# Three edits at the end of a mixture-of-experts kernel: one final store, a w2 load in three pieces, and eight small reads of x

## The chip, the cores and the metric

The kernel runs on one core of one Trainium2 chip. The metric is device time in microseconds (us) of one execution. A core has a matmul engine (PE), three engines for elementwise work (DVE, ACT, and POOL, which here mostly issues DMAs), a queue engine (SP), and 16 DMA engines that move data between the chip's main memory (HBM) and its on-chip memory (SBUF). DMAs issued from SP and ACT go to hardware queues (q1 and q10 in the profile), those issued from POOL to a software queue (q0).

## What is computed

Eight experts, each a two-layer network on its own 256 tokens:

```
x: [8, 256, 512]   w1: [8, 512, 2048]   w2: [8, 2048, 512]   all float32
h   = maximum(x @ w1, 0)
out = h @ w2            # [8, 256, 512] float32
```

## The kernel before

The loads convert float32 to bf16 on the way, so all weight traffic is issued by POOL (`load_w1`, L82; `load_w2`, L88). Weights come in whole experts: a w1 of one expert and a w2 of one expert are 4 MB each in HBM and 2 MB in SBUF. x comes with two plain loads on SP for experts 0 and 1 (L67, cast by DVE at L69), and then in pairs of experts from POOL (L74). The list `loads` holds the order: w1 and w2 of expert 0, x of 2 and 3, w1 and w2 of expert 1, and so on; L104 puts w1 of the last expert ahead of w2 of the one before it. `issue` takes from that list as far as it is told to. The order of PE's and POOL's instructions is the order in which the code issues them (`manual_schedule`, L179); those of the other engines are placed by a scheduler.

Two w2 loads are cut along the rows that a partition holds (`PIECES`, L55): expert 6 into 8 and 8 rows of 512, expert 7 into 4, 4, 4, 2 and 2. A row here is a slice of k of the second matmul. Each partition's part of a piece is one packet, so a piece is 128 packets, eight for each DMA engine, and each DMA leaves sixteen completion marks, one for each engine.

For each expert, PE transposes x (`prepare`, L119), runs layer 1 (`layer1`, L135: 64 matmuls of 128 x 256 into PSUM, with ReLU by ACT at L142), and layer 2 (`layer2`, L161: 32 matmuls of 128 x 512 into two PSUM tiles, one for each half m of the tokens). For experts 6 and 7 layer 2 goes over k outside and m inside, so that it can begin with the first piece of w2. Layer 1 of expert 7 runs ahead of layer 2 of expert 6.

DVE copies the results out of PSUM (L172); the very last one, m = 1 of expert 7, is copied by ACT (L170). Outputs are gathered in SBUF by groups of experts: 0 to 2, 3 to 6, and 7 alone. The group of 0 to 2 is stored from POOL in the midst of the loads (`store`, L92), that of 3 to 6 from POOL after all loads (L201, 2 MB). Expert 7 is stored in two halves: m = 0 from SP after DVE's copy, m = 1 from ACT after ACT's copy (L175). On SP's queue stand only the two x loads and that half store.

Of the kernel before, what the change touches and what calls it, by code (L numbers as in the profile page):

```python
# [9 lines left out]
FP32 = mybir.dt.float32  # L10
# [4 lines left out]
def kernel(  # L15
# [7 lines left out]
    nc = tc.nc  # L23
    P = 128
    E, C, H = x.shape
    F = w1.shape[2]
    MC = C // P
# [8 lines left out]
    out_v = out.rearrange("e (p mo) k -> e p (mo k)", mo=MC)  # L36
# [4 lines left out]
    x_pool = ctx.enter_context(tc.tile_pool(name="x_pool", bufs=2))  # L41
# [10 lines left out]
    identity = const.tile([P, P], BF16, name="identity")  # L52


    PIECES = {E - 2: [8, 8], E - 1: [4, 4, 4, 2, 2]}  # L55


    GROUPS = [(0, 1, 2), (3, 4, 5, 6), (7,)]
    GROUP = {e: g for g in GROUPS for e in g}
# [3 lines left out]
    xbs, w1s, w2s, outs = {}, {}, {}, {}  # L63
# [20 lines left out]
    def load_w2(e):  # L84
        w2s[e] = t = w2_pool.tile([P, K2 * H], BF16, name="w2_sb")
        k = 0
        for n in PIECES.get(e, [K2]):
            nc.gpsimd.dma_start(t[:, k * H:(k + n) * H], w2_v[e, :, k * H:(k + n) * H])  # L88
            k += n

    def store(g):
        nc.gpsimd.dma_start(  # L92
            og_v[:, g[0]:g[-1] + 1, :], outs[g][:].rearrange("p e m h -> p e (m h)")
        )
# [11 lines left out]
    def issue(upto):  # L106
        while loads:
            f, e = loads[0]
            if (f, e) not in upto:
                break  # L110
            loads.pop(0)
            f(e)

    def prepare(e):
        xb = xbs[e]
        xt_ps = psum_t.tile([P, K1, MC, P], BF16, name="xt_ps")
        for ko in range(K1):
            for mo in range(MC):
                nc.tensor.transpose(xt_ps[:, ko, mo, :], xb[:, mo, :, ko], identity[:])  # L119
        xT = xT_pool.tile([P, K1, C], BF16, name="xT")  # L120
        nc.vector.tensor_copy(  # L121
            xT[:].rearrange("p k c -> p (k c)"),
            xt_ps[:].rearrange("p k m q -> p (k m q)"),
        )
        return xT

    def layer1(e, xT):
        w1_r = w1s[e][:].rearrange("p (ko q j) -> p ko q j", ko=K1, j=K2)
        hT = hT_pool.tile([P, K2, C], BF16, name="hT")
        for pr in range(K2 // 2):  # L130
            h_ps = psum_h.tile([P, 2, C], FP32, name="h_ps")
            for s in range(2):
                j = pr * 2 + s
                for ko in range(K1):
                    nc.tensor.matmul(  # L135
                        h_ps[:, s, :],
                        w1_r[:, ko, :, j],
                        xT[:, ko, :],
                        start=(ko == 0),
                        stop=(ko == K1 - 1),  # L140
                    )
            nc.scalar.activation(  # L142
                hT[:, pr * 2:pr * 2 + 2, :].rearrange("p a c -> p (a c)"),
                h_ps[:].rearrange("p a c -> p (a c)"),
                mybir.ActivationFunctionType.Relu,
            )
        return hT

    def layer2(e, hT):
        last = e == E - 1  # L150
        g = GROUP[e]
        if e == g[0]:
            outs[g] = out_pool.tile([P, len(g), MC, H], FP32, name=f"out_sb{g[0]}")
        out_sb = outs[g][:, e - g[0]]
        o_ps = [psum_o.tile([P, H], FP32, name="o_ps") for _ in range(MC)]
        if e in PIECES:
            order = [(k, m) for k in range(K2) for m in range(MC)]
        else:
            order = [(k, m) for m in range(MC) for k in range(K2)]
        for k, m in order:  # L160
            nc.tensor.matmul(  # L161
                o_ps[m][:],
                hT[:, k, m * P:(m + 1) * P],
                w2s[e][:, k * H:(k + 1) * H],
                start=(k == 0),
                stop=(k == K2 - 1),
            )
            if k == K2 - 1:
                if last and m == 1:
                    nc.scalar.copy(out_sb[:, m, :], o_ps[m][:])  # L170
                else:
                    nc.vector.tensor_copy(out_sb[:, m, :], o_ps[m][:])  # L172
                if last:
                    eng = nc.scalar if m == 1 else nc.sync
                    eng.dma_start(out_v[e, :, m * H:(m + 1) * H], out_sb[:, m, :])  # L175

    load_x_first(0)
    load_x_first(1)
    with tc.manual_schedule(engines={mybir.EngineType.PE, mybir.EngineType.Pool}):  # L179
        f, e = loads.pop(0)  # L180
        f(e)
        make_identity(nc, identity)
        f, e = loads.pop(0)
        f(e)
        make_identity(nc, identity)
        issue([(load_w2, 0), (load_x, X_GROUPS[0]), (load_w1, 1), (load_w2, 1), (load_w1, 2)])
        xT = prepare(0)
        for e in range(E - 1):
            issue(
                [(load_w2, e + 2), (load_w1, e + 3), (load_w1, E - 1), (load_w2, e + 1)]  # L190
                + [(load_x, g) for g in X_GROUPS if g[0] <= e + 4]
            )
            for g in GROUPS[:-2]:
                if g[-1] == e - 1:
                    store(g)
            hT = layer1(e, xT)
            xT = prepare(e + 1)
            if e == E - 2:
                hT_last = layer1(E - 1, xT)
            layer2(e, hT)  # L200
        store(DEFER)  # L201
        layer2(E - 1, hT_last)
# [28 lines left out]
```

## Time and profile before

| | us |
|---|---|
| median of 4 runs (lowest, highest) | 182.69 (182.31, 182.73) |
| the profiled execution | 182.43 |
| its span, first to last instruction | 180.6 |
| PE busy with matmuls | 131.4 (73%) |
| DVE, ACT, POOL busy | 17.1, 40.1, 16.5 |
| layer 2, matmul of 128 x 512, count and busy | 256, 56.7 |
| loads of w, 2 MB each in SBUF: median from issue to landing | 61.4 |
| HBM read, written | 71.30 MB, 4.19 MB |

Each number of the profile is from one execution, the profiled one. Busy time is time in which an engine had an instruction in work; a line of the timeline gives start, duration, engine, source line and operation, and in brackets how long the engine sat idle before it and what ended that wait. The page's row "DMA" gives for 40 equal slices of the span the busy share of the 16 DMA engines in tenths, and "PEclk" the share of its full clock that PE was granted.

### The profile page before, as it was taken

How to read it: one execution, taken by the hardware profiler on the slowest of the kernel's cores; microseconds unless marked ns; L12 is line 12 of the kernel's file. 1: busy time of each engine (PE TensorE's matmuls, PEld its weight loads, DVE VectorE, ACT ScalarE, POOL GpSimd, SP SyncE). 2: the span in 40 equal slices, each digit the busy share in tenths (PEclk: the TensorE clock that was granted, in tenths of full speed). 3: DMA queues.
4: the chain of work that ended last, by engine and by line, in shares of the span. 5: the costliest groups of instructions: out<-in, count | busy, mean ns of one | idle time of the engine just before them, and what ended most of it. 6: DMA issues, size and time to landing. Idle time of an engine off the chain costs nothing.

```text
span 180.6 us, 1861 instructions
## 1 busy us (share of the span) xinstructions
PE 131.4 (73%) x832; PEld 92.1 (51%) x832; DVE 17.1 (9%) x25; ACT 40.1 (22%) x66; POOL 16.5 (9%) x34
## 2 busy tenths in 40 slices
PE   0206999169894999349894999539995997887960
PEld 0105874059543874139642884127942897833420
DVE  0300011100111011100111002100031001000210
ACT  2001440016300450006300360003600264600010
POOL 7601011010000023000201002010100101000100
PEclk9999999969999699969999699975999699999996
DMA  6998999899999989989998999999899989999995
GB/s 220 245 229 181 229 232 218 189 232 232 200 207 232 225 173 241 232 185 221 232 229 185 225 196 232 210 232 232 185 221 232 229 180 366 220 207 214 208 395 211
DMA packets 5351, 40.48 MB, mean 224 GB/s; under 512 B 480, under 2 KB 480, under 8 KB 3296
## 3 DMA queue, kind: packets, MB, share of 16 engines
q0 software_dynamic: 4768, 38.80, 97.7%
q1 hardware_dynamic: 432, 1.31, 2.0%
q10 hardware_dynamic: 144, 0.26, 0.4%
q8 instruction: 6, 0.10, 0.2%
q14 instruction: 1, 0.01, 0.0%
HBM read 71.30 MB, written 4.19 MB: 418 GB/s over the span
## 4 chain that ended last, share of the span: by engine, by line
DMA 70%; another core or an unknown queue 11%; PE 11%; POOL 2%; issue 2%; ACT 0%; POOLq 0%
DMA w_sb<-in_w_dram 46%; DMA xb<-in_x_dram 24%; PE o_ps L161 6%; PE h_ps L135 5%; POOL w_sb L82 1%; POOL w_sb L88 1%; POOL xb L74 0%; ACT out_sb L170 0%; POOL identity masks.py:199 0%; POOL identity masks.py:197 0%; PE xt_ps L119 0%; POOLq masks.py:199 0%; POOLq L88 0%; POOLq L215 0%
## 5 line engine op out<-in xcount | busy, mean ns | idle before, releaser
L135 PE MATMUL h_ps<-xT,w_sb 128*128 128x256 bf16 x512 | 70.9, 310 | 33.3 <-DMA w_sb<-in_w_dram 33.3
L135 PEld LDWEIGHTS <-w_sb 128*128 128x128 bf16 x512 | 63.1, 150 | 42.6 <-DMA w_sb<-in_w_dram 36.7
L142 ACT ACTIVATE hT<-h_ps 128x512 bf16<-128x512 f32 x64 | 38.2, 597 | 117.8 <-PE h_ps L135 117.8
L161 PE MATMUL o_ps<-w_sb,hT 128*128 128x512 bf16 x256 | 56.7, 379 | 5.0 <-DMA w_sb<-in_w_dram 5.0
L161 PEld LDWEIGHTS <-hT 128*128 128x128 bf16 x256 | 24.9, 98 | 34.5 <-issue 6.2
L172 DVE COPY out_sb<-o_ps 128x512 f32<-128x512 f32 x15 | 10.3, 691 | 59.0 <-PE o_ps L161 59.0
L121 DVE COPY xT<-xt_ps 128x1024 bf16<-128x1024 bf16 x8 | 5.5, 691 | 94.3 <-PE xt_ps L119 94.3
L88 POOL DMA_DIRECT2D w_sb<-in_w_dram x13 | 7.0, 536 | 76.0 <-DMA w_sb<-in_w_dram 73.8
L119 PE MATMUL xt_ps<-identity,xb 128*128 128x128 bf16 x64 | 5.3, 230 | 4.9 <-DVE xb L69 4.9
L82 POOL DMA_DIRECT2D w_sb<-in_w_dram x8 | 4.8, 600 | 29.8 <-PE h_ps L135 17.8
L119 PEld LDWEIGHTS <-xb 128*128 128x128 bf16 x64 | 4.7, 117 | 4.9 <-DVE xb L69 4.9
L74 POOL DMA_DIRECT2D xb<-in_x_dram x3 | 2.1, 717 | 28.0 <-PE xt_ps L119 28.0
L170 ACT COPY out_sb<-o_ps 128x512 f32<-128x512 f32 x1 | 0.6, 586 | 16.6 <-PE o_ps L161 16.6
L92 POOL DMA_DIRECT2D out_dram<-out_sb x2 | 1.5, 756 | 18.7 <-DVE out_sb L172 17.7
L69 DVE CAST xb<-x_sb 128x1024 bf16<-128x1024 f32 x2 | 1.4, 694 | 4.7 <-DMA x_sb<-in_x_dram 4.7
L142 ACT ACT_TABLE_LOAD x1 | 1.3, 1283 | 0.7 <-PEq L215 0.7
masks.py:199 POOL TENSOR_SCALAR_AFFINE_SELECT identity<-identity 128x128 bf16<-128x128 bf16 x2 | 0.6, 287 | 0.2
masks.py:197 POOL MEMSET identity<- 128x128 bf16 x2 | 0.4, 223 | 0.0
L215 POOL MEMSET const-float32-0.0<- 128x1 f32 x1 | 0.1, 98 | 0.2 <-issue 0.2
L215 POOL MEMSET const-bfloat16-1.0<- 128x1 bf16 x1 | 0.1, 101 | 0.0
L215 POOL MEMSET const-uint8-127<- 128x1 uint8 x1 | 0.1, 101 | 0.0
L215 POOL MEMSET const-float32-1.0<- 128x1 f32 x1 | 0.1, 98 | 0.0
## 6 DMA issues: line engine op xcount, KB each, us to landing
w_sb<-in_w_dram POOLq DMA_DIRECT2D x14, 2048.0 KB, 61.4
w_sb<-in_w_dram POOLq DMA_DIRECT2D x2, 1024.0 KB, 57.5
out_dram<-out_sb POOLq DMA_DIRECT2D x1, 2048.0 KB, 9.9
xb<-in_x_dram POOLq DMA_DIRECT2D x3, 512.0 KB, 43.9
out_dram<-out_sb POOLq DMA_DIRECT2D x1, 1536.0 KB, 64.5
w_sb<-in_w_dram POOLq DMA_DIRECT2D x3, 512.0 KB, 47.8
x_sb<-in_x_dram SPq DMA_DIRECT2D x2, 512.0 KB, 3.8
w_sb<-in_w_dram POOLq DMA_DIRECT2D x2, 256.0 KB, 27.5
```

Of the source, the lines that this page charges most:

```text
L69: nc.vector.tensor_copy(b[:].rearrange("p m q k -> p (m q k)"), t[:])
L74: nc.gpsimd.dma_start(t[:].rearrange("p e m q k -> p e (m q k)"), xg_v[:, g[0]:g[0] + 2, :])
L82: nc.gpsimd.dma_start(w1s[e][:], w1_v[e])
L88: nc.gpsimd.dma_start(t[:, k * H:(k + n) * H], w2_v[e, :, k * H:(k + n) * H])
L92: nc.gpsimd.dma_start(og_v[:, g[0]:g[-1] + 1, :], outs[g][:].rearrange("p e m h -> p e (m h)"))
L119: nc.tensor.transpose(xt_ps[:, ko, mo, :], xb[:, mo, :, ko], identity[:])
L121: nc.vector.tensor_copy(xT[:].rearrange("p k c -> p (k c)"), xt_ps[:].rearrange("p k m q -> p (k m q)"),)
L135: nc.tensor.matmul(h_ps[:, s, :], w1_r[:, ko, :, j], xT[:, ko, :], start=(ko == 0), stop=(ko == K1 - 1),)
L142: nc.scalar.activation(hT[:, pr * 2:pr * 2 + 2, :].rearrange("p a c -> p (a c)"), h_ps[:].rearrange("p a c -> p (a c)"), mybir.ActivationF ...
L161: nc.tensor.matmul(o_ps[m][:], hT[:, k, m * P:(m + 1) * P], w2s[e][:, k * H:(k + 1) * H], start=(k == 0), stop=(k == K2 - 1),)
L170: nc.scalar.copy(out_sb[:, m, :], o_ps[m][:])
L172: nc.vector.tensor_copy(out_sb[:, m, :], o_ps[m][:])
```

## The change

Three edits. Expert 7's w2 is loaded in pieces of 8, 4 and 4 rows. Its output is stored by one DMA from SP, after both halves are copied. And once expert 4's layer 2 is issued, `small_loads` takes a buffer of the pool that x's first two loads used, writes 16 rows of it with a DVE copy out of expert 4's result, and then issues eight reads from SP into the same rows: 15 rows of x (2 KB each), then 14, and so on down to 8. Each read waits for the one before it, the first for the DVE copy. The change is described as reads on 15 down to 8 DMA engines. What is read is used by nothing.

```diff
-    PIECES = {E - 2: [8, 8], E - 1: [4, 4, 4, 2, 2]}
+    PIECES = {E - 2: [8, 8], E - 1: [8, 4, 4]}
...
                 else:
                     nc.vector.tensor_copy(out_sb[:, m, :], o_ps[m][:])
-                if last:
-                    eng = nc.scalar if m == 1 else nc.sync
-                    eng.dma_start(out_v[e, :, m * H:(m + 1) * H], out_sb[:, m, :])
+        if last:
+            nc.sync.dma_start(out_v[e], out_sb.rearrange("p m h -> p (m h)"))
+
+    def small_loads(e):
+        t = x_pool.tile([P, MC * H], FP32, name="x_sb")
+        nc.vector.tensor_copy(t[:16, 0:H], outs[GROUP[e]][:16, e - GROUP[e][0], 0])
+        for k in range(15, 7, -1):
+            nc.sync.dma_start(t[:k, 0:H], x[0, :k, :])
...
             layer2(e, hT)
+            if e == 4:
+                small_loads(e)
         store(DEFER)
         layer2(E - 1, hT_last)
```

As built, DVE's small copy stands between expert 4's two copies out of PSUM, and SP's queue holds the two x loads, the eight reads and the final store, in that order. Counts and order on PE are unchanged; POOL issues two DMAs fewer, ACT one fewer.

## The prediction

> **What bounds the kernel now.** I read the page's row of DMA shares and its list of queues first, then the timeline of the last 30 us, the waits of SP's queue, and last the trace's records of single DMA packets and of the sixteen completion marks that each DMA leaves.
>
> ```profile
> PEclk9999999969999699969999699975999699999996
> DMA  6998999899999989989998999999899989999995
> ...
> q0 software_dynamic: 4768, 38.80, 97.7%
> q1 hardware_dynamic: 432, 1.31, 2.0%
> q10 hardware_dynamic: 144, 0.26, 0.4%
> q8 instruction: 6, 0.10, 0.2%
> ```
>
> The DMA engines are busy from the first slice to the last, nearly all of it (97.7%) with the software queue that POOL issues to: every load of w1, w2 and grouped x, and the two grouped stores. Work that is not on this path is free as long as it stays off it. The timeline of the tail:
>
> ```profile
> 158.74 3.61 PE L161 MATMUL o_ps<-w_sb,hT 128*128 128x512 bf16 x16 [1.34 <-DMA w_sb<-in_w_dram]
> ...
> 163.61 7.07 PE L161 MATMUL o_ps<-w_sb,hT 128*128 128x512 bf16 x32 [1.25 <-DMA w_sb<-in_w_dram]
> ...
> 168.63 0.76 POOL L92 DMA_DIRECT2D out_dram<-out_sb  x1 [17.66 <-DVE out_sb L172]
> 170.98 3.61 PE L161 MATMUL o_ps<-w_sb,hT 128*128 128x512 bf16 x16 [0.31 <-DMA w_sb<-in_w_dram]
> ...
> 174.42 0.69 DVE L172 COPY out_sb<-o_ps 128x512 f32<-128x512 f32 x1 [6.09 <-PE o_ps L161]
> 174.63 0.59 ACT L170 COPY out_sb<-o_ps 128x512 f32<-128x512 f32 x1 [16.59 <-PE o_ps L161]
> 175.13 0.35 SPq L175 DMA_DIRECT2D out_dram<-out_sb  x1
> 175.25 0.37 ACTq L175 DMA_DIRECT2D out_dram<-out_sb  x1
> ```
>
> PE and the copies are done at 175.2, yet the span is 180.6. The page's chain follows PE and ACT here, but the packets say what the last 5 us are: the grouped store of experts 3 to 6 (2 MB, issued at 168.63) stands in each engine's queue behind the last w2 piece. It drains on the first engine at 176.45 and on the last at 178.12; only then do the final stores' packets run there, and they end at 179.42. So the end is one DMA engine's queue, not PE.
>
> That queue is not equally long everywhere. The sixteen marks of the last w2 piece fall between 171.8 and 173.5. Following each engine's packets by their period shows why: each of the six q8 packets (16 KB of instructions) hit a different engine, and each put that engine back by about 1.1 us for good. At the end ten engines lie 0 to 0.6 us behind the first, two 1.2 to 1.3, and four 1.6 to 1.7. These four set the end; the ten have at least 1.0 us to spare.
>
> **The change, part by part**, on those four engines.
>
> Last w2 as 8, 4, 4 instead of 4, 4, 4, 2, 2. Packet periods on one engine: 606 ns in an 8-row piece (from expert 6's halves), 304 in a 4-row piece, 154 in a 2-row piece, eight packets each, plus 21 ns for the mark. Before: 3 x (8 x 304 + 21) + 2 x (8 x 154 + 21) = 9.87 us. After: (8 x 606 + 21) + 2 x (8 x 304 + 21) = 9.78 us. Gain 0.1 us.
>
> One store of 512 KB instead of two of 256 KB. Before, 16 packets of 2 KB at 80 ns and two marks of 6 ns: 1.29 us. After, 8 packets of 4 KB at the 155 ns of the grouped store and one mark: 1.25 us. Gain 0.05 us. ACT loses an issue of 0.37 us, which nothing waits for.
>
> What these two edits push back is PE's end. The 8-row piece lands at 163.56 + 4.87 = 168.43 (before, the first 4-row piece was there at 166.02), and all 32 matmuls come after it: 32 x 0.221 (7.07 us / 32) = 7.1, so PE ends at 175.6, not 174.6. Copies to 176.2; then one SP issue that waits for both. SP's x load issued at 0.74 had its first packet at 1.75, and the final store's first packet came 1.33 us after its issue, so the store's packets are at the engines 177.2 to 177.6. The cover is the grouped store, which keeps the four late engines busy until 178.0. It covers by 0.4 us; if that cover were gone, each further microsecond of PE would be a microsecond of time. The early engines run dry for up to 1 us, and end about 179.1, still ahead.
>
> The small reads. DVE's copy of 16 x 512 lies in a DVE idle of 2.76 us between its copies at 111.93 and 115.38: nothing. Then eight reads on SP, of 15 down to 8 rows of 2 KB, each waiting for the one before, since they write the same tile. Queued behind them on SP is only the final store:
>
> ```profile
> SPq L175 <- DVE out_sb L172: 173.5, 1, 173.5
> SPq L226 <- DMA out_dram<-out_sb: 3.9, 3, 2.8
> ```
>
> SP has nothing to do from 1.6 to 175.1. From issue to landing the HBM transfers on the hardware queues take 3.8 us (x, 512 KB) to 4.5 (256 KB store). At 4.5 the eight end at 112.6 + 36 = 149. They may take up to (176.2 - 112.6) / 8 = 7.9 us each before the final store is late. So SP is covered.
>
> What is not covered is engine time: each read puts one 2 KB packet and a mark into a queue that is never empty. If one row goes to one engine, always counted from the same engine, eight engines get all eight reads and the other eight get 7 down to none; if the change doesn't do what its description says and the rows go round, it is 92 / 16 = 5.75 each. The price of one insertion is not in the trace. From below: a 2 KB packet and its mark in the final stores, 0.086 us, with no gap at the handover. From above: an instruction packet put its engine back by 1.09 us where an equal amount of the same queue takes half of 1.208, so 0.49 us of insertion, plus 0.09: 0.58 us. Nothing below zero: the reads remove no packet. I take 0.09, since the final stores are the nearer row in kind and size; eight of them are 0.7 us, and by the upper end 4.6.
>
> Does it land on a late engine? Six of sixteen are late, four of them decide, and the trace doesn't name engines. If the late ones lay at random, all four would miss the eight fully loaded engines in 70 of 1820 draws; if six late ones lie side by side, in about one start in five. So I take it that a deciding engine gets seven or eight. The last w2 piece, PE's end and the grouped store are then late by the same 0.7, so the cover of 0.4 stays.
>
> Sum: -0.1 - 0.05 + 0.7 = +0.55 us. The profiled execution took 182.43 (span 180.6 and 1.83 around it), which gives 182.98; the median of four runs is 182.69, 0.26 above it, and carries to **183.24**.
>
> The Trainium skill ("DMA: Bandwidth & Descriptors", section "Why a DMA increments its semaphore by 16 and not by 1") says that a hardware-queue DMA on k engines uses the lowest-numbered k, which would make engines 0 to 7 the fully loaded ones; no row here shows an engine's number. The same page ("Queues, rings and completion order") says that an engine takes turns between its queues packet by packet. The row disagrees in part: on the four late engines the grouped store's packets ran on unbroken from 176.5 to 178.0 while the final stores already ran elsewhere. By the rule the reads slip in and the sum stands; by the row they would wait for the software queue to run dry, which is the third rival.
>
> **Rivals.**
>
> 1. Not slower: the late engines are those with few reads. Its place is the gap between engines: an engine with 0.6 us of lag can take (1.66 - 0.6) / 8 = 0.13 us a read before it becomes the last. If the four late engines hold none to three of the reads (at most 0.26 us) and an insertion costs under 0.13, the sum is -0.15 to +0.1: 182.5 to 182.8. It decides as soon as no late engine has more than three. For it: the ten others do have 1.0 us to spare. Against: the odds above.
>
> 2. Insertion costs like the instruction packets, 0.2 to 0.58 us a read: +1.5 to +4.5, so 184.2 to 187.2. For it: the only packets seen to break into the software queue cost this. Against: they were 16 KB, and handovers between queues elsewhere took 6 ns.
>
> 3. The reads wait until the software queue is dry, at about 178, and the final store stands behind them on SP: eight at 2.5 us (3.8 less 1.25 of transfer) and a store of 4: about 20 us more, 203. For it: three handovers in this trace (x to software queue at 4.6, grouped store to SP's store, SP's to ACT's on the late engines) all ran one queue dry first. Against: the instruction packets got in amid a backlog.
>
> 4. The tail's cover fails (late first packet or a slow last piece): +0.2 to +0.8, on top of the sum; to 184.0.
>
> 5. Faster by more than the edits add up to: the disturbance at 145 to 147.5, where every engine lost 0.04 to 0.9 us without a cause in this trace, falls elsewhere. Up to -0.6: 182.1.
>
> **How the numbers follow.** Forecast 45%, with rival 4 in it 8% more; rival 1 19%; rival 2 14%; rival 3 5%; rival 5 9%. A difference of 0.2% is 0.37 us, about what measuring this kernel can tell from none. Slower by more: forecast less its lower edge (38 of 45), rivals 2, 3, 4: 65%; rounded to 0.62 for what rival 1 may take. Faster by more: rival 5, and rival 1 where packets and store save twice what I gave: 0.16. Within: 0.22. The forecast's own range is 182.9 to 183.9. The whole reaches down to 182.2, which holds rival 1, and up to 184.8, which holds the cheaper half of rival 2; rival 3, rival 2's upper half and some of rival 5 are left out.
>
> **What would show it.** In the new profile: SP's queue with eight issues spaced under 8 us and ended before 150; the marks of the last w2 piece spread wider by 0.7 us and later than 173.5 by 0.6; PE's end at 176.2 or so, with no wait for DMA before its last matmuls; one final store whose packets on the last engine follow the grouped store's without a gap. The forecast is wrong if those marks are no later than before (rival 1), later by over 1.3 us (rival 2), or if the eight issues run past 176 (rival 3).

## The result

| | before | after |
|---|---|---|
| median of all runs, us (runs) | 182.57 (63) | 182.94 (43) |
| ratio, 95% interval | | 1.0021 [1.0015, 1.0027] |
| the profiled execution, us | 182.43 | 183.33 |
| its span, us | 180.6 | 181.5 |

The change makes the kernel 0.37 us slower; the forecast was 0.55 slower, which lies above the interval of 0.27 to 0.49 us. The profiled execution after is the slowest of its 43 runs, so the two spans differ by more than the kernels do: the sizes below come from the ratios, the profiles show only where things lie.

The page's DMA row and queue list of the kernel after:

```profile
DMA  6999999999999999999999999999999999999994
...
q0 software_dynamic: 4480, 38.80, 97.0%
q1 hardware_dynamic: 616, 1.76, 2.6%
q8 instruction: 6, 0.10, 0.2%
```

The software queue moved the same 38.80 MB in 288 packets fewer (the 4- and 2-row pieces), q10 (ACT's queue) is gone, and q1 holds the reads and the one store. Still no slice in which the DMA engines rest.

The timeline of the tail after (start, duration, engine, line, operation, idle before it):

```profile
164.33 3.61 PE L161 MATMUL o_ps<-w_sb,hT 128*128 128x512 bf16 x16 [1.25 <-DMA w_sb<-in_w_dram]
...
169.20 7.07 PE L161 MATMUL o_ps<-w_sb,hT 128*128 128x512 bf16 x32 [1.25 <-DMA w_sb<-in_w_dram]
169.35 0.76 POOL L92 DMA_DIRECT2D out_dram<-out_sb  x1 [38.13 <-DVE out_sb L172]
176.09 0.69 DVE L172 COPY out_sb<-o_ps 128x512 f32<-128x512 f32 x1 [7.03 <-PE o_ps L161]
176.30 0.59 ACT L170 COPY out_sb<-o_ps 128x512 f32<-128x512 f32 x1 [17.59 <-PE o_ps L161]
176.91 0.38 SPq L174 DMA_DIRECT2D out_dram<-out_sb  x1
```

All 32 matmuls of expert 7 now run without a gap behind the 8-row piece, and PE ends at 176.27 in place of 174.59. The store's first packet is at 177.78. SP's timeline and waits after:

```profile
0.74 0.85 SPq L67 DMA_DIRECT2D x_sb<-in_x_dram  x2
113.40 43.00 SPq L180 DMA_DIRECT2D x_sb<-in_x_dram  x8
176.91 0.38 SPq L174 DMA_DIRECT2D out_dram<-out_sb  x1
```

```profile
SPq L180 <- DVE x_sb L178: 109.3, 1, 109.3
SPq L180 <- DMA x_sb<-in_x_dram: 42.9, 8, 6.7
SPq L174 <- DVE out_sb L172: 20.4, 1, 20.4
```

The eight reads are issued from 113.4 to 156.1, 5.1 to 7.0 us apart. Each leaves as many completion marks as it has rows, 15 down to 8, one on each engine that it uses. Then SP waits 20.4 us for the copies: the final store doesn't wait for the reads.

The completion marks show who sets the end. Each line holds the sixteen marks of one DMA in order of time, in us, taken from the trace's records:

```
before, grouped store   176.87 176.99 177.00 177.04 177.05 177.21 177.27 177.28 177.32 177.40 178.05 178.12 178.39 178.42 178.46 178.48
before, ACT's store     178.14 178.28 178.29 178.30 178.31 178.49 178.56 178.59 178.64 178.70 179.32 179.38 179.66 179.70 179.73 179.76
after, grouped store    177.24 177.32 177.39 177.52 177.59 177.60 177.65 177.67 177.70 177.93 178.56 178.91 178.92 178.94 178.97 179.10
after, final store      179.38 179.40 179.41 179.42 179.45 179.46 179.47 179.48 179.52 179.56 179.79 180.14 180.17 180.18 180.20 180.35
```

Ten engines and six late ones, before and after. After, the ten finish the final store together (179.38 to 179.56): they had run dry and waited for its first packet. The late ones finish one store's length, 1.24 us, behind their own grouped store: they never ran dry. The last of them sets the end, 0.6 us later than before in these two executions.

### The profile page after: what moved, and what is told of

It reads as the page before. It is cut to its first block, busy times and chain, and to the rows that moved or that the text cites. A ratio compares the mean times of both kernels' runs of the same rounds, so it can differ in the third digit from the quotient of the medians.

```text
span 181.5 us, 1870 instructions
## 1 busy us (share of the span) xinstructions
PE 127.2 (70%) x832; PEld 89.7 (49%) x832; DVE 17.5 (10%) x26; ACT 40.1 (22%) x66; POOL 15.4 (8%) x32
## 3 DMA queue, kind: packets, MB, share of 16 engines
q0 software_dynamic: 4480, 38.80, 97.0%
## 4 chain that ended last, share of the span: by engine, by line
PE 61%; DMA 19%; another core or an unknown queue 15%; POOL 1%; issue 1%; ACT 0%; POOLq 0%
PE h_ps L135 32%; PE o_ps L161 27%; DMA w_sb<-in_w_dram 19%; PE xt_ps L119 1%; POOL xb L74 0%; POOL w_sb L82 0%; ACT out_sb L170 0%; POOL identity masks.py:199 0%; POOL identity masks.py:197 0%; POOL w_sb L88 0%; POOLq masks.py:199 0%; POOLq L222 0%
## 5 line engine op out<-in xcount | busy, mean ns | idle before, releaser
L135 PE MATMUL h_ps<-xT,w_sb 128*128 128x256 bf16 x512 | 66.4, 297 | 35.1 <-DMA w_sb<-in_w_dram 35.1
L135 PEld LDWEIGHTS <-w_sb 128*128 128x128 bf16 x512 | 60.6, 148 | 42.4 <-DMA w_sb<-in_w_dram 38.5
L88 POOL DMA_DIRECT2D w_sb<-in_w_dram x11 | 5.9, 535 | 57.9 <-DMA w_sb<-in_w_dram 55.7
L82 POOL DMA_DIRECT2D w_sb<-in_w_dram x8 | 4.8, 596 | 31.3 <-PE h_ps L135 18.3
```

Of the source, the lines that this page charges most:

```text
L82: nc.gpsimd.dma_start(w1s[e][:], w1_v[e])
L135: nc.tensor.matmul(h_ps[:, s, :], w1_r[:, ko, :, j], xT[:, ko, :], start=(ko == 0), stop=(ko == K1 - 1),)
```

## The experiments

Times are ratios to the kernel before on the same chip, with 95% intervals; 0.001 is 0.18 us.

**The tail edits alone**: the call of `small_loads` left out.

```diff
-            if e == 4:
-                small_loads(e)
```

> The changed kernel without the eight reads: 8, 4, 4 pieces and one store alone. Theory (one late DMA engine's queue sets the end; the reads are the cost, the tail edits save packets): 0.15 us faster than before. Rival A (the tail edits are the cost: PE now ends about 1.1 us later and the store comes late to engines that run dry; the reads fall on engines with time to spare): 0.3 to 0.4 us slower than before, like the whole change. In the trace by the theory: PE ends near 175.6, the store's first packets near 177.2, its last ones on the late engines right behind the grouped store.

Measured 0.9987 [0.9975, 0.9999]. The same kernel again, with the last runs below:

> The tail edits alone once more, for a second interval and on the same chip as the others of this call: 0.1 to 0.3 us faster than before.

Measured 0.9993 [0.9979, 1.0006]. The mean of the two is 0.18 us faster; rival A, which wanted 0.3 to 0.4 slower, falls. The tail in its first profile:

```profile
168.20 7.07 PE L161 MATMUL o_ps<-w_sb,hT 128*128 128x512 bf16 x32 [1.25 <-DMA w_sb<-in_w_dram]
...
175.92 0.35 SPq L174 DMA_DIRECT2D out_dram<-out_sb  x1
```

PE ends at 175.27, 0.7 us later than in the profile before, and the kernel is no slower for it.

**The reads alone**: the kernel before, with `small_loads` and its call.

> The kernel before with the eight reads alone. Theory: +0.5 to +0.7 us (a late engine gets seven or eight reads at 0.09 us). Rival A: 0 to +0.1 us. Rival B (a read costs more than 0.09 us on an engine, and the late engines get only some of them): +0.5 as well, but the q0 packets of one engine show gaps of over 0.2 us where a read goes in.

Measured 1.0025 [1.0015, 1.0036], +0.46 us. So the reads are the cost, and tail edits and reads add up: -0.18 + 0.46 = +0.28 is within the interval of +0.37, at its lower end. A read does not leave gaps of over 0.2 us: see the marks of the next run.

**Reads on all engines**: eight reads of 16 rows, tail edits kept.

```diff
-        for k in range(15, 7, -1):
+        for k in [16] * 8:
```

> The changed kernel with eight reads of 16 rows each, so that all sixteen engines get all eight. Theory: the deciding engines already got seven or eight, so the time is that of the changed kernel or up to 0.1 us more: +0.4 to +0.6 us against before. Rival B (the deciding engines got only some of the reads): 0.3 us or more above the changed kernel, +0.7 or more against before.

Measured 1.0039 [1.0026, 1.0052], +0.71, which is 0.89 over the tail edits alone. That is 0.34 above the change itself, as rival B wants it; the two intervals just touch (1.0026 and 1.0027), so the times alone don't quite exclude my theory. The price of one read can be read off the marks of the 2 MB loads. With the tail edits alone a load into which no instruction packet falls takes 9.68 or 9.69 us on nearly every engine, mark to mark; in this run 9.78 where one read falls into it and 9.87 where two do. So a read costs 0.09 to 0.095 us on its engine, and eight cost 0.70 to 0.75.

**Reads on half of the engines**: eight reads of 8 rows.

```diff
-        for k in range(15, 7, -1):
+        for k in [8] * 8:
```

> The changed kernel with eight reads of 8 rows each, so that only eight engines get any. Theory: if the deciding engines are among those eight, the same as the changed kernel, +0.4 us against before; if none of them is, the reads are free and the time is that of the tail edits alone, 0.15 us faster than before. In the trace the marks of a DMA late in the run must fall into two halves 0.7 us apart, apart from the lag of the instruction packets.

Measured 1.0012 [1.0002, 1.0021], +0.22, which is 0.40 over the tail edits alone: neither full nor free. The marks say why. When the reads begin, four engines are late, by 1.09, 1.09, 1.34 and 1.39 us; over the load of expert 5's w2, into which two reads fall, two of them take 9.69 and two 9.87. So two of the four get the reads, the less late ones, and two get none. At the end:

```
grouped store, rows of 8   177.00 177.14 177.15 177.18 177.46 177.51 177.52 177.53 177.58 178.02 178.12 178.16 178.22 178.30 178.69 178.72
```

Two engines stand out at 178.7. Without their eight reads (0.70 to 0.75 us) they would be at about 178.0, and the last would be the one at 178.30. In this execution the cost is therefore the 0.42 by which they pass it. The time agrees (0.40, to within some 0.25), but the reads on four engines below weaken that agreement.

**Reads on twelve engines**: eight reads of 12 rows, edited like the two before.

> The changed kernel with eight reads of 12 rows each. Eight on all sixteen engines gave +0.95 us over no reads, eight on eight engines +0.46. If reads fall on the engines counted from one fixed end and the late engines that eight rows spare are among the next four: +0.95 over no reads, so +0.7 us against before. If they are among the last four: +0.46, so +0.2 against before. If the engines of a read rotate: three quarters of 0.95, +0.5 against before.

Measured 1.0041 [1.0026, 1.0056], +0.75, 0.93 over the tail edits: as much as on all sixteen. In its marks three of the four engines late by then take 9.87 us over the load with two reads, and one 9.69. The intervals alone would also allow that the engines rotate (+0.5); the marks don't, since of these four three got each of the first three reads and the fourth none. Which engines are late need not be the same as in the execution with 8 rows (see the account of the prediction), so the step from two to three of four doesn't place a given engine.

**Reads on four engines**: eight reads of 4 rows.

> The changed kernel with eight reads of 4 rows each. Theory (a read costs 0.115 us on each engine that it uses and matters only where it falls on a late engine): either the late ones among the first eight engines are among the first four, then as with eight rows, +0.2 us against before, or they aren't, then the reads are free and the time is that of the tail edits alone, 0.2 us faster than before. Rival (the reads cost something by being there at all, through the memory or SP): more than the tail edits alone in any case, in proportion to the rows: +0.46 x 4 / 8 = 0.23 over them.

Measured 1.0013 [1.0001, 1.0026], against 0.9993 [0.9979, 1.0006] for the tail edits on the same chip, 0.36 us more. The intervals touch. Against the mean of the two tail runs, the baseline of the other runs here, it is 0.42 more, as much as with 8 rows. In the marks none of the four engines late by then gets a read (9.69 us a load), so by the theory these reads should have been free; its profiled execution ends its grouped store at 178.42, the two of the tail edits at 178.10 and 178.60. Whether four engines' reads cost anything is not settled. The rival of a cost by being there, forecast at 0.23, is not excluded, and some of the cost of the other runs may be of that kind.

**Sixteen reads of 16 rows**, from expert 1 on.

```diff
-        for k in range(15, 7, -1):
+        for k in [16] * 16:
...
-            if e == 4:
+            if e == 1:
```

> Sixteen reads of 16 rows, from expert 1 on, tail edits kept. Theory: the cost goes with the number of reads on the deciding engine: 16 x 0.115 = 1.84 us over the tail edits alone, +1.6 against before. Rival (a fixed cost, or one that later work takes back): about what eight such reads cost, +0.7 against before. Issues about 6 us apart, so that SP is through by 160.

Measured 1.0081 [1.0068, 1.0094], +1.48, so 1.66 over the tail edits alone, 0.104 us a read, to within some 0.02. The cost goes with the number and nothing later takes it back; that all of it is a fixed cost is out.

**The cover at the tail taken away**: tail edits, no reads, last w2 in two pieces of 8.

```diff
-    PIECES = {E - 2: [8, 8], E - 1: [8, 4, 4]}
+    PIECES = {E - 2: [8, 8], E - 1: [8, 8]}
```

> The tail edits without reads, and the last w2 in two pieces of 8: 16 matmuls (3.6 us) stand behind the last piece, so PE ends near 176.9 and the store's packets come near 178.6, when the grouped store has left even the late engines (178.0). Theory (the late engines' grouped store covers PE's lateness, by some 0.4 to 1 us): the cover is gone, and the time is 0.4 to 0.9 us above the tail edits alone, which were 0.24 us faster than before: +0.2 to +0.7 us. Rival (PE's end doesn't matter, the store's packets alone do): 0.3 us faster than before.

Measured 1.0028 [1.0013, 1.0043], +0.51, 0.69 over the tail edits with 8, 4, 4. Its tail:

```profile
173.04 3.61 PE L161 MATMUL o_ps<-w_sb,hT 128*128 128x512 bf16 x15 [1.45 <-DMA w_sb<-in_w_dram]
...
176.47 0.69 DVE L172 COPY out_sb<-o_ps 128x512 f32<-128x512 f32 x1 [8.64 <-PE o_ps L161]
176.69 0.58 ACT L170 COPY out_sb<-o_ps 128x512 f32<-128x512 f32 x1 [19.11 <-PE o_ps L161]
177.30 0.35 SPq L174 DMA_DIRECT2D out_dram<-out_sb  x1
```

PE ends at 176.65, the store's first packet is at 178.14, when the grouped store has left even the late engines (177.99). All sixteen marks of the final store lie within 0.18 us, 179.75 to 179.93: now the store's issue sets the end for every engine.

**The tail edits one by one.** The pieces alone, two half stores kept:

> The kernel before with expert 7's w2 in pieces of 8, 4, 4 alone, two half stores kept. Theory: 0.1 us faster than before (9.78 us of packets on each engine in place of 9.87), or the same; PE ends about 1 us later and this costs nothing. Rival (the saving of the tail edits is all in the single store): no difference.

Measured 0.9997 [0.9984, 1.0011]. The single store alone, pieces 4, 4, 4, 2, 2 kept:

> The kernel before with one final store alone, pieces 4, 4, 4, 2, 2 kept. Theory: 0.05 us faster than before, so no difference that can be told, and up to 0.1 more if a second store has a cost of its own after its last packet. Rival (the saving of the tail edits is all here): 0.2 us faster.

Measured 0.9995 [0.9978, 1.0013]. Both are too small for these intervals; neither theory nor rival is told apart here.

**The reads put later**: after expert 5 in place of expert 4.

> The changed kernel with its reads put after expert 5 in place of expert 4. The reads then start near 135 and, at about 6 us each, end near 178 to 183, while SP's final store is ready at 176.9. Theory (SP's queue is covered only as long as the reads are through before 176): the store is late by 1 to 6 us and the time goes up by as much, less the 1.1 us for which engines are still busy then: +1 to +5 us against before. Rival (the reads get quicker as the pieces get smaller, and are through in time): +0.4, as in the changed kernel.

Measured 1.0034 [1.0019, 1.0048], +0.62, not told apart from the change. SP's timeline:

```profile
135.63 36.55 SPq L180 DMA_DIRECT2D x_sb<-in_x_dram  x8
177.19 0.38 SPq L174 DMA_DIRECT2D out_dram<-out_sb  x1
```

My expectation was wrong: the reads get quicker as the software queue's packets get smaller, 5.8 and 6.4 us apart at first, 4.3 to 4.8 among the last four. What shrinks is mostly the time after a read's first packet: on its engine the read's mark often goes out only after one more packet of the software queue, 1.30 us behind the read where these are 16 KB, 0.4 in the 4-row pieces. The last issue is over at 172.2, and the store goes out when the copies are done. SP's cover holds even with the reads put 22 us later.

## Why the prediction was right, and where it was off

**What sets the end**: right. One late DMA engine's queue does, before and after; the grouped store's cover for PE's lateness is shown by the run that takes it away (0.69 us). The cover was wider than the 0.4 of the prediction: after the change the final store's first packet is at 177.78, 0.87 us after its issue, and the grouped store's last packet on the latest engine ends at 178.77, 1.0 us behind it. So rival 4 falls.

**The tail edits**: -0.15 forecast, -0.18 as the mean of two runs. PE's end with the reads was forecast at 175.6 plus the reads' delay, 176.2 or so, and lay at 176.27. That closeness is partly luck: two profiles of one kernel, the tail edits, have PE's end 0.47 us apart (175.27 and 175.74).

**Price of one read**: right. 0.09 taken, 0.09 to 0.095 by the marks, 0.104 by sixteen reads to within 0.02. The upper bound of 0.58, from the instruction packets, is far off for a 2 KB packet: rival 2 falls.

**Which engines get them**: this is the step that was mis-sized. "So I take it that a deciding engine gets seven or eight", 0.7 us; the reads cost 0.46 alone and 0.55 on top of the tail edits, the worth of five to six. With 8 rows two of the first four late engines get all eight, but they are not the latest ones, and the lead of some 0.3 us that the latest had on them swallows nearly half of the price. In the changed kernel's own marks three of the four engines that are late when the reads begin get both the 15-row and the 14-row read, and the fourth, the latest then, gets the 15-row read and not the next. At the end of that execution the last engine is one that took neither the 9-row nor the 8-row read (4.867 us for each 8-row piece of expert 6, where the two late ones that took them have 4.961); those two end 0.2 us before it.

Nor need the late engines be the same in every execution. The six instruction packets that make engines late last 893, 893, 948, 945, 935 and 975 ns in the profile with 8 rows, 948, 945, 935, 975, 974 and 961 in that with 12, and 974, 962, 893, 893, 951 and 945 in the changed kernel's. All fourteen profiles show the same round of eight lengths to within some 15 ns, begun at one of four places. If a length goes with an engine, which fits the late engines that got reads in these three profiles but was not tested, other engines are late in other executions, and the "five to six" is a mean over them. Rival 1 named the mechanism, time to spare, but wanted the late engines to have at most three reads.

**SP's queue**: the reads were through at 161.7, not 149: 6.1 us from issue to landing, not at most 4.5. The margin I gave, 7.9 us each, held, so it cost nothing.

**The reads behind the software queue** (rival 3): wrong. They broke into a full queue, the first packet of each 3.3 to 4.0 us after its issue, where SP's first x load needed 1.0. That agrees in kind with the rule of the Trainium skill ("DMA: Bandwidth & Descriptors", section "Queues, rings and completion order") that an engine takes turns between its queues packet by packet. The turn doesn't come at once, though, and the wait is not a number of packets: with the reads put later it is 3.3 to 3.4 us too where the software queue runs packets of 0.3 us. What the other 2.3 us are spent on is not shown. The unbroken grouped store on the late engines, from which I argued the rival, fits such a wait: SP's half store was issued at 175.13, and the last of these engines ran dry at 178.12, 3.0 us later.

**What I said would show it**: the last w2 piece's marks are later by 0.56 us (174.07 for 173.51), as forecast, but one profile of each can't carry this: the two profiles of the tail edits alone have that mark at 173.07 and 173.55. That they spread wider by 0.7 was wrong (1.82 for 1.71): early engines got reads as well as late ones.

## What to carry to other kernels

When a kernel keeps its DMA engines full, compare the engines with each other before pricing an extra transfer: the sixteen marks of each DMA show which engines are late, and by these marks an extra packet costs its own time on the latest and nothing on the others until they catch up with it; the reads on four engines leave open whether there is a small cost besides. Which engines are late may change from one execution to the next, so one profile is not enough to place a transfer by. Work that ends before the last queue has drained, here PE by 0.7 us, may be made later for free. The fastest version here is the tail edits without the reads, by 0.18 us against before, at the edge of what these intervals can tell.

## What the runs showed that I had not expected

Most 2 MB loads in mid-run take 9.68 or 9.69 us on an engine without a read or an instruction packet, to 0.01 us, but the one ahead of the first grouped store (w1 of expert 7) took 9.70 to 10.36 on the earliest engine in the fourteen profiles. For one and the same kernel, the tail edits, it took 9.91 in one profile and 10.22 in the other, and the spans were 180.2 and 180.7. So part of the scatter between executions may arise there, but not all: the profile with the shortest such load, 9.70 (the single store alone), has a span of 181.3, and in it one engine is 2.3 us behind the first at the end. An 8 KB instruction packet on q14 falls into this load in every profile, that one too, so it alone doesn't explain the loss; its cause was not found.
